# Convolution copies through memory on GpSimd's queue, with a block's write issued ahead of the reads of the block before

## The chip, the core and the metric

The kernel runs on one core of a Trainium2 chip, as one launch. The metric is the device time of one execution in microseconds; a run's figure is the median of several executions. SP, ACT and POOL can start DMAs, each in the order of its own instructions; an instruction that waits for a semaphore holds everything behind it on its engine.

## What is computed

A trunk of two layers over 256 positions of 1024 channels, in float32. Each layer is a SwiGLU FFN, a mixer and a second FFN, all with modulation and gates from a conditioning vector. The mixer of layer 0 is attention, that of layer 1 a convolution module, and the change lies in that one:

```python
def conformer_conv(h, w_pw1, b_pw1, w_dw, b_dw, ln_g, ln_b, w_pw2, b_pw2):
    u = h @ w_pw1 + b_pw1                      # 1024 -> 2048
    a, g = jnp.split(u, 2, axis=-1)
    u = a * jax.nn.sigmoid(g)
    u = depthwise_causal_conv(u, w_dw) + b_dw  # width 31, per channel
    u = jax.nn.silu(layer_norm(u, ln_g, ln_b))
    return u @ w_pw2 + b_pw2
```

(The call of the depthwise convolution is shortened here.)

## The kernel before

**Weights.** All weights come through one stream of loads, 512 KB (0.524 MB) each, 128 x 1024 float32, into a ring of six buffers `raw` (`RAW = 6`). `issue` (L191) starts a load on SP. `step` (L208) uses up the oldest one: for a weight, ACT rounds it to `whi` (L245, one load ahead of the step) and DVE subtracts to get `wlo` (L220); for a piece of the adaLN matrix DVE folds it into an accumulator (L284, L286). Then `step` issues the load six places on, which SP can start when the buffer is free. The pairs `whi`, `wlo` have a ring of six units (`RING = 6`), two loads to a unit; `high_part` (L233) refuses a unit while the one six places back still has uses, and the step then ends. `need(unit)` makes steps until a unit is there; `block()` (L258) makes as many as the quota of `take(n)` allows. A product with a weight is three matmuls per tile, hi.hi, lo.hi, hi.lo (L664 to L666).

**The convolution module** (`conv`, L1000) works on eight blocks of 128 channels. I number its loads from the first one of `pw1`: 0 to 15 are `pw1` (two per block), 16 to 23 `pw2`, 24 to 31 a piece of the adaLN matrix, from 32 on the weights of the last FFN. "Step n" uses up load n, and frees the buffer for load n + 6.

For a block b:

- `U(b)` (L1024): two products on TensorE, 48 matmuls of 256 columns, with a `need` and a `block()` ahead of them. Blocks 0 to 3 are done in another form (`UT`, `across`) before the loop.
- `glu(b)` (L1061): ACT takes the sigmoid of one half (L1065), DVE multiplies it into the row buffer `ub[b % 4]` (L1066), 288 columns with a margin of zeros.
- `spread(b)` (L1070): DMAs build `R[b]`. Its partitions 32 j to 32 j + 31 hold, for j = 0 to 3, the four groups of 32 channels side by side, shifted by j columns. That is 16 copies from on-chip memory to on-chip memory, each of 32 runs of 284 floats (1,136 bytes), half on SP and half on POOL. `R` has four buffers, so that `spread(b + 4)` waits for `C(b)`.
- `wide(b)` (L1017): POOL makes the weights `wd[b]` of the taps (three buffers, so that `wide(b + 3)` waits for `C(b)`).
- `C(b)` (L1079): 32 matmul instructions of 256 columns (64 rows in the trace) give the convolution, ACT moves it to `v` (L1089).
- `VT(b)` (L1093): two transposes of `v` into the accumulators `y` of the layer norm.

The order is written out by hand (L1149 to L1207); each engine executes its own instructions in that order. In the loop (L1178) it is U(b+4), glu(b+4), C(b), spread(b+4), wide(b+3), VT(b-1). After it come C(4) to C(7) with halves of 128 columns, interleaved with transposes, the moments, the norm, `swish` (four transposes and an activation), `put` (split into `hh` and `hl`) and the output product `O`. `run_sums(True)` makes the two column sums of an adaLN vector on TensorE (L340).

The last FFN's first loads are used up in the blocks after U(7): 32 to 35, where the ring of weight units refuses more.

Of the kernel before, what the change touches and what calls it, by code (L numbers as in the profile page):

```python
# [8 lines left out]
F32 = mybir.dt.float32  # L9
# [5 lines left out]
P = 128  # L15
# [41 lines left out]
class Trunk:  # L57
    def __init__(self, ctx, tc, a):
        self.tc, self.nc, self.a = tc, tc.nc, a

        def pool(name, bufs=1, **kw):
            return ctx.enter_context(tc.tile_pool(name=name, bufs=bufs, **kw))

        self.const = pool("const")
        self.tiny = pool("tiny", 2)
        pool("pad").tile([P, 256], F32, name="pad")
        self.rawp = pool("rawp", RAW)
        self.hlp = pool("hlp", RING)
        self.keep = pool("keep")
        self.two = pool("two", 2)  # L70
        self.ps = pool("ps", 1, space=bass.MemoryType.PSUM)
        self.vecs = {(l, s, k): Vec(l, s, k) for l in range(2) for s in range(3) for k in range(3)}
        self.sums, self.open, self.pend, self.naccs = [], [], [], 0
        self.phase = 0
        self.ss, self.rs, self.zs = {}, {}, {}
        self.quota = self.credit = 0
        self.plan()
# [189 lines left out]
    def take(self, n=None):  # L267
        self.quota = PUMP[self.phase] if n is None else n
# [731 lines left out]
    def conv(self, cp, before, after):  # L1000
        nc, a = self.nc, self.a
        b1, bdw = self.col["b1"], self.col["bdw"]
        lng, lnb = self.col["lng"], self.col["lnb"]
        cols, take = self.cols, self.take
# [5 lines left out]
        ub = [cp.tile([P, 288], F32, name=f"ub{i}") for i in range(4)]  # L1010
# [6 lines left out]
        def wide(b):  # L1017
            wd[b] = cp.tile([P, 8, 4, 32], F32, name="wd", tag="wd", bufs=3)
            nc.gpsimd.tensor_tensor(
                wd[b], self.w2[:, :, 4 * b : 4 * b + 4].unsqueeze(3).to_broadcast([P, 8, 4, 32]),  # L1020
                mask.unsqueeze(1).unsqueeze(1).to_broadcast([P, 8, 4, 32]), op=ALU.mult,
            )

        def U(b):  # L1024
            unit = self.pw1[b]
            self.need(unit)
            self.block()
            us[b] = self.bank("u")
            for s in range(2):
                out = us[b][:, s * T : s * T + T]  # L1030
                for k in range(KT):
                    cs = slice(k * 256 + s * P, k * 256 + s * P + P)
                    self.mm3(out, unit.hi[:, cs], unit.lo[:, cs], self.hh[:, k, :], self.hl[:, k, :], k == 0, k == KT - 1)
            unit.uses -= 1
# [26 lines left out]
        def glu(b):  # L1061
            ps = us.pop(b)
            u = ub[b % 4]
            sg = cp.tile([P, T], F32, name="sg", tag="sg", bufs=2)
            nc.scalar.activation(sg, ps[:, T:], AF.Sigmoid, bias=cols[:, b1 + 8 + b : b1 + 9 + b])  # L1065
            nc.vector.scalar_tensor_tensor(  # L1066
                u[:, 30:286], ps[:, 0:T], cols[:, b1 + b : b1 + b + 1], sg, op0=ALU.add, op1=ALU.mult
            )

        def spread(b):  # L1070

            u = ub[b % 4]
            R[b] = cp.tile([P, 4, 284], F32, name="R", tag="R", bufs=4)
            for g in range(4):
                for j in range(4):
                    eng = nc.sync if (g + j) % 2 else nc.gpsimd
                    eng.dma_start(R[b][32 * j : 32 * j + 32, g, :], u[32 * g : 32 * g + 32, j : j + 284])  # L1077

        def C(b, t0=0, n=T):  # L1079
            if ("v", b) not in us:  # L1080
# [85 lines left out]
        UT(w[1][:, 256:], 2, 1)  # L1166
        across(0, 1, e, 0), across(1, 1, e, 256)
        e = evac(w[1])
        glu(0), spread(0), wide(0)
        UT(w[3][:, 256:], 3, 1)  # L1170
        f = evac(w[3])
        across(2, 0, e, 0), across(2, 1, e, 256)
        glu(1), spread(1), wide(1)
        across(3, 0, f, 0), across(3, 1, f, 256)
        glu(2), spread(2), wide(2)
        glu(3), spread(3)
        take(PUMP_LOOP)
        for b in range(4):  # L1178
            U(b + 4)
            glu(b + 4)  # L1180
            C(b)
            spread(b + 4), wide(b + 3)
            if b:
                VT(b - 1)
                if b == 1:
                    nc.vector.tensor_tensor(b2, b2, gate, op=ALU.mult)
                else:
                    x = self.x[b - 2]
                    nc.vector.tensor_tensor(x, x, b2, op=ALU.add)
        nc.scalar.activation(warm, self.mhalf, AF.Silu)  # L1190
        self.block()
        C(4), wide(7), VT(3)
        self.need(self.pw2[3])
        take(5)
        C(5, 0, P), VT(4), self.block(), C(6, 0, P), VT(5, (0,)), C(7, 0, P), VT(6, (0,))
        C(5, P, P), VT(7, (0,)), moments(0), norm(0, 0), norm(0, 1)
        take(0)
        C(6, P, P), VT(5, (1,)), C(7, P, P), VT(6, (1,)), swish(0, 0), VT(7, (1,)), moments(1), put(0, 0)
        self.run_sums(True)
        swish(0, 1), norm(1, 0), put(0, 1), norm(1, 1)  # L1200
        O(0, 0), swish(1, 0), O(0, 1), put(1, 0), swish(1, 1), put(1, 1), take()
        O(0, 2), O(0, 3)
# [60 lines left out]
```

## Time and profile before

| | us |
|---|---|
| median of 3 runs | 1058.22 |
| lowest and highest run | 1056.94, 1062.69 |
| the profiled execution | 1057.27 |
| its span | 1055.5 |
| TensorE busy | 1020.3 (97%) |
| DVE, ACT, POOL busy | 785.3, 489.6, 86.8 |

The span is what the trace covers; the execution's own time is 1.77 us longer. All rows below are of that execution, in us from the span's start. The row of a matmul ends where its end is modelled, so rows on TensorE overlap a little. The convolution's U(4) begins at 759.88 us, and its first output product at 839.88 us.

### The profile page before, as it was taken

The page shows a single profiled execution, that of the slowest core. Times are in us where ns is not written, and L with a number is a line of the kernel's source. Part 1 is how long each engine was busy: PE and PEld are TensorE (multiplying, and loading weights), DVE is VectorE, ACT ScalarE, POOL GpSimd, SP SyncE. Part 2 cuts the span into 40 slices and gives each one's busy share as a digit, 9 for nine tenths or more (in the row PEclk, how much of TensorE's full clock was granted, in tenths as well). Part 3 has the DMA queues.
Part 4 walks back from the last instruction along what each step waited for, and adds up shares of the span by engine and source line. Part 5 has one row for each costly group of instructions (what it writes and reads, how often), then busy time and mean ns, then how long its engine had stood idle before and what let it go on. Part 6 is the DMA issues. An engine that isn't in the chain of part 4 may idle for free.

```text
span 1055.5 us, 14925 instructions
## 1 busy us (share of the span) xinstructions
PE 1020.3 (97%) x5510; PEld 826.7 (78%) x5510; DVE 785.3 (74%) x1165; ACT 489.6 (46%) x763; POOL 86.8 (8%) x149
## 2 busy tenths in 40 slices
PE   8999999999999999999999999999995899999998
PEld 5778787877776788878878878888984688888886
DVE  5679888978997798878578878776747669556643
ACT  3454444555685544444454444454621356434420
POOL 3000000002210000000020000000484200000000
PEclk9999999999999999999999999999998999999999
DMA  8989999948676399999739889894667427776711
GB/s 299 316 273 333 305 341 321 324 140 284 220 241 194 106 329 313 308 309 315 233 105 315 290 297 312 276 307 136 193 201 227 159 80 259 259 234 193 231 40 40
DMA packets 186812, 254.92 MB, mean 242 GB/s; under 512 B 10437, under 2 KB 136166, under 8 KB 186740
## 3 DMA queue, kind: packets, MB, share of 16 engines
q1 hardware_dynamic: 183856, 250.88, 72.1%
q0 software_dynamic: 2736, 3.04, 1.0%
q8 instruction: 43, 0.70, 0.3%
q14 instruction: 29, 0.24, 0.1%
q10 hardware_dynamic: 148, 0.06, 0.0%
HBM read 248.24 MB, written 1.05 MB: 236 GB/s over the span
## 4 chain that ended last, share of the span: by engine, by line
PE 79%; DVE 7%; DMA 5%; ACT 3%; issue 3%; POOL 2%; SPq 1%; DVEq 0%; ACTq 0%; POOLq 0%
PE u L666 14%; PE u L664 14%; PE u L665 14%; PE y L664 10%; PE y L666 10%; PE y L665 10%; DMA raw<-in_ffn_w_in_dram 2%; DMA raw<-in_ada_w_dram 2%; DVE wlo L220 2%; PE m L742 2%; ACT whi L245 1%; POOL R L1077 1%; PE m L1085 1%; ACT p L893 1%; DVE x L601 1%
## 5 line engine op out<-in xcount | busy, mean ns | idle before, releaser
L220 DVE TENSOR_TENSOR wlo<-raw,whi 128x1024 fp32r<-128x1024 f32 x320 | 389.2, 1244 | 51.1 <-ACT whi L245 50.8
L245 ACT ACTIVATE whi<-raw 128x1024 fp32r<-128x1024 f32 x320 | 329.1, 1055 | 178.1 <-DMA raw<-in_ffn_w_in_dram 96.2
L664 PE MATMUL u<-whi,hh 128*128 128x512 f32 x672 | 266.7, 397 | 1.2 <-ACT hh L587 1.2
L666 PE MATMUL u<-whi,hl 128*128 128x512 f32 x672 | 263.1, 391 | 0.0
L665 PE MATMUL u<-wlo,hh 128*128 128x512 f32 x672 | 261.8, 390 | 0.0
L286 DVE SCALAR_TENSOR_TENSOR acc<-raw,sc,acc 128x512 f32<-128x512 f32 x224 | 168.0, 750 | 6.7 <-DMA raw<-in_ada_w_dram 1.7
L666 PEld LDWEIGHTS u<-whi,hl 128*128 128x128 f32 x672 | 126.1, 188 | 29.6 <-DVE hl L588 1.7
L664 PEld LDWEIGHTS u<-whi,hh 128*128 128x128 f32 x672 | 126.2, 188 | 28.7 <-ACT hh L587 2.9
L665 PEld LDWEIGHTS u<-wlo,hh 128*128 128x128 f32 x672 | 126.4, 188 | 25.0
L664 PE MATMUL y<-whi,gh 128*128 128x512 f32 x352 | 138.5, 393 | 0.2 <-ACT gh L750 0.2
L666 PE MATMUL y<-whi,gl 128*128 128x512 f32 x352 | 137.3, 390 | 0.0
L665 PE MATMUL y<-wlo,gh 128*128 128x512 f32 x352 | 137.1, 389 | 0.0
L664 PE MATMUL y<-whi,hh 128*128 128x512 f32 (+1 forms) x256 | 96.9, 379 | 0.2 <-ACT hh L934 0.2
L666 PE MATMUL y<-whi,hl 128*128 128x512 f32 (+1 forms) x256 | 93.9, 367 | 0.0
L665 PE MATMUL y<-wlo,hh 128*128 128x512 f32 (+1 forms) x256 | 93.5, 365 | 0.0
L751 DVE TENSOR_TENSOR gl<-m,gh 128x512 fp32r<-128x512 f32 (+1 forms) x48 | 31.0, 647 | 83.7 <-ACT gh L750 83.5
L750 ACT ACTIVATE gh<-m 128x512 fp32r<-128x512 f32 (+1 forms) x48 | 27.0, 563 | 131.9 <-PE m L742 131.8
L712 ACT ACTIVATE sg<-u 128x256 f32<-128x256 f32 x84 | 32.1, 383 | 106.6 <-PE u L666 106.6
L664 PEld LDWEIGHTS y<-whi,gh 128*128 128x128 f32 x352 | 66.1, 188 | 15.7 <-ACT sg L712 1.7
L666 PEld LDWEIGHTS y<-whi,gl 128*128 128x128 f32 x352 | 66.1, 188 | 14.4 <-DVE gl L751 0.4
L665 PEld LDWEIGHTS y<-wlo,gh 128*128 128x128 f32 x352 | 66.1, 188 | 13.4
L620 POOL TENSOR_TENSOR r<-v,mhalf 128x1 f32<-128x1 f32 x12 | 6.6, 554 | 671.9 <-DVE v L619 671.9
(169 smaller groups left out, 944.6 us busy)
## 6 DMA issues: line engine op xcount, KB each, us to landing
raw<-in_ffn_w_in_dram SPq DMA_DIRECT2D x164, 512.0 KB, 5.1
raw<-in_ada_w_dram SPq DMA_DIRECT2D x144, 512.0 KB, 5.1
raw<-in_ffn_w_out_dram SPq DMA_DIRECT2D x88, 512.0 KB, 5.3
raw<-in_attn_w_qkv_dram SPq DMA_DIRECT2D x24, 512.0 KB, 4.9
raw<-in_conv_w_pw_dram SPq DMA_DIRECT2D x24, 512.0 KB, 5.1
raw<-in_ffn_w_in_dram SPq DMA_DIRECT2D x24, 256.0 KB, 5.7
raw<-in_attn_w_o_dram SPq DMA_DIRECT2D x8, 512.0 KB, 4.3
gate<-in_ada_b_dram SPq DMA_DIRECT2D x6, 512.0 KB, 6.7
```

Of the source, the lines that this page charges most:

```text
L220: (eng or nc.vector).tensor_tensor(lo, raw, hi.bitcast(F32), op=ALU.subtract)
L245: self.nc.scalar.activation(hi, self.like(self.raws[i], hi), AF.Copy)
L286: nc.vector.scalar_tensor_tensor(dst, raw[:, i, :], self.sc[:, k : k + 1], dst, op0=ALU.mult, op1=ALU.add)
L601: nc.vector.tensor_tensor(x[:, s], x[:, s], tmp, op=ALU.add)
L664: nc.tensor.matmul(out, lh, rh, start=start, stop=False)
L665: nc.tensor.matmul(out, lh, rl, start=False, stop=False)
L666: nc.tensor.matmul(out, ll, rh, start=False, stop=stop)
L712: nc.scalar.activation(sg, ps[:, 0:256], AF.Silu)
L742: nc.tensor.transpose(ps[:, o : o + P], g[:, t, k * P : k * P + P], self.ident)
L750: nc.scalar.activation(hi, src, AF.Copy)
L751: nc.vector.tensor_tensor(lo, src, hi.bitcast(F32), op=ALU.subtract)
L893: nc.scalar.activation(p[:, c0:c1], p[:, c0:c1], AF.Exp, bias=st[:, t : t + 1], scale=-1.0, accum_out=st[:, 2 + t : 3 + t],)
```

## The change

`spread(b)` now reads from memory. A new `park(b)` writes the row buffer (128 x 288) to a tile in DRAM, one of eight, on POOL; `spread(b)` is four DMAs on POOL, one for each shift j, each of which reads 32 x 4 x 284 floats, that is 128 runs of 1,136 bytes. A read waits for its write to land. `park(b + 1)` is issued ahead of `spread(b)`. SP has no part in it any more. The order of the blocks is rewritten for that: U(b+5) and glu(b+5) come ahead of C(b) in the loop, C(5) is done whole, one `block()` and one `take` go, and the column sums move ahead of the first `swish`.

```diff
+        self.dram = pool("dram", space=bass.MemoryType.DRAM)
...
+        drams = {}
+
+        def park(b):
+
+            drams[b] = self.dram.tile([P, 288], F32, name=f"d{b}")
+            nc.gpsimd.dma_start(drams[b], ub[b % 4])
+
         def spread(b):
 
-            u = ub[b % 4]
+            d = drams[b]
             R[b] = cp.tile([P, 4, 284], F32, name="R", tag="R", bufs=4)
-            for g in range(4):
-                for j in range(4):
-                    eng = nc.sync if (g + j) % 2 else nc.gpsimd
-                    eng.dma_start(R[b][32 * j : 32 * j + 32, g, :], u[32 * g : 32 * g + 32, j : j + 284])
+            for j in range(4):
+                src = bass.AP(tensor=d.tensor, offset=d.offset + j, ap=[[288, 32], [288 * 32, 4], [1, 284]])
+                nc.gpsimd.dma_start(R[b][32 * j : 32 * j + 32, :, :], src)
...
-        glu(0), spread(0), wide(0)
+        glu(0), park(0)
...
-        glu(1), spread(1), wide(1)
+        glu(1), park(1), spread(0), wide(0)
         across(3, 0, f, 0), across(3, 1, f, 256)
-        glu(2), spread(2), wide(2)
-        glu(3), spread(3)
+        glu(2), park(2), spread(1), wide(1)
+        glu(3), park(3), spread(2), wide(2)
         take(PUMP_LOOP)
+        U(4)
+        glu(4)
         for b in range(4):
-            U(b + 4)
-            glu(b + 4)
+            if b < 3:
+                U(b + 5)
+            park(b + 4), spread(b + 3)
+            if b:
+                wide(b + 2)
+            if b < 3:
+                glu(b + 5)
             C(b)
-            spread(b + 4), wide(b + 3)
             if b:
                 VT(b - 1)
...
         nc.scalar.activation(warm, self.mhalf, AF.Silu)
-        self.block()
+        spread(7), wide(6)
         C(4), wide(7), VT(3)
         self.need(self.pw2[3])
-        take(5)
-        C(5, 0, P), VT(4), self.block(), C(6, 0, P), VT(5, (0,)), C(7, 0, P), VT(6, (0,))
-        C(5, P, P), VT(7, (0,)), moments(0), norm(0, 0), norm(0, 1)
+        self.block()
+        C(5), VT(4), C(6, 0, P), VT(5), C(7, 0, P), VT(6, (0,))
         take(0)
-        C(6, P, P), VT(5, (1,)), C(7, P, P), VT(6, (1,)), swish(0, 0), VT(7, (1,)), moments(1), put(0, 0)
+        C(6, P, P), VT(7, (0,)), moments(0), norm(0, 0), norm(0, 1)
+        C(7, P, P), VT(6, (1,))
         self.run_sums(True)
+        VT(7, (1,)), swish(0, 0), moments(1), put(0, 0)
         swish(0, 1), norm(1, 0), put(0, 1), norm(1, 1)
```

SP's queue around U(4) to U(6), before; `raw` is a load (the first row is load 18), `R` a copy of `spread`:

```order
L205 DMA raw_6757<-in_conv_w_pw2_dram 128x1024
L1077 DMA R_6793<-ub0_6532 32x284 x8
L205 DMA raw_6813<-in_conv_w_pw2_dram 128x1024
L205 DMA raw_6819<-in_conv_w_pw2_dram 128x1024
L1077 DMA R_6856<-ub1_6533 32x284 x8
L1077 DMA R_6883<-ub2_6534 32x284 x8
L1077 DMA R_6905<-ub3_6535 32x284 x8
L205 DMA raw_6923<-in_conv_w_pw2_dram 128x1024
L205 DMA raw_6929<-in_conv_w_pw2_dram 128x1024
L205 DMA raw_6933<-in_conv_w_pw2_dram 128x1024
L205 DMA raw_6939<-in_ada_w_dram 128x2x512
L205 DMA raw_6943<-in_ada_w_dram 128x2x512
```

And now, from the same load on:

```order
L206 DMA raw_6759<-in_conv_w_pw2_dram 128x1024
L206 DMA raw_6798<-in_conv_w_pw2_dram 128x1024
L206 DMA raw_6804<-in_conv_w_pw2_dram 128x1024
L206 DMA raw_6880<-in_conv_w_pw2_dram 128x1024
L206 DMA raw_6886<-in_conv_w_pw2_dram 128x1024
L206 DMA raw_6890<-in_conv_w_pw2_dram 128x1024
L206 DMA raw_6896<-in_ada_w_dram 128x2x512
```

The 64 copies are gone from SP, and its loads follow each other.

POOL from the first block on, before (`ub` are the row buffers, `wd` the weights of the taps):

```order
L1077 DMA R_6793<-ub0_6532 32x284 x8
L1019 TENSOR_TENSOR wd_6810<-w2_4906,mask_6528 128x1024
L1077 DMA R_6856<-ub1_6533 32x284 x8
L1019 TENSOR_TENSOR wd_6873<-w2_4906,mask_6528 128x1024
L1077 DMA R_6883<-ub2_6534 32x284 x8
L1019 TENSOR_TENSOR wd_6900<-w2_4906,mask_6528 128x1024
L1077 DMA R_6905<-ub3_6535 32x284 x8
L1077 DMA R_7032<-ub0_6532 32x284 x8
L1019 TENSOR_TENSOR wd_7049<-w2_4906,mask_6528 128x1024
L1077 DMA R_7148<-ub1_6533 32x284 x8
```

And now, with the DRAM tiles `d0` to `d7`:

```order
L1076 DMA d0_6795<-ub0_6534 128x288
L1076 DMA d1_6841<-ub1_6535 128x288
L1084 DMA R_6843<-d0_6795 32x4x284 x4
L1020 TENSOR_TENSOR wd_6848<-w2_4908,mask_6530 128x1024
L1076 DMA d2_6858<-ub2_6536 128x288
L1084 DMA R_6860<-d1_6841 32x4x284 x4
L1020 TENSOR_TENSOR wd_6865<-w2_4908,mask_6530 128x1024
L1076 DMA d3_6870<-ub3_6537 128x288
L1084 DMA R_6872<-d2_6858 32x4x284 x4
L1020 TENSOR_TENSOR wd_6877<-w2_4908,mask_6530 128x1024
L1076 DMA d4_7013<-ub0_6534 128x288
L1084 DMA R_7015<-d3_6870 32x4x284 x4
```

Eight copies of a block have become one write and four reads, and the write of a block stands ahead of the reads of the block before.

TensorE at the end of the convolution, before: the first row is the second half of C(6), L1085 and L1099 are C and VT, L1122 the transposes of `swish`, L340 the column sums, the last row the first output product:

```order
L1085 MATMUL m_7654<-R_7282,wd_7432 32x128 x32
L1099 MATMUL y_7535<-ident_141,v_7498 128x128
L1085 MATMUL m_7689<-R_7415,wd_7490 32x128 x32
L1099 MATMUL y_7535<-ident_141,v_7537 128x128
L1122 MATMUL m_7724<-ident_141,z_7650 128x128 x4
L1099 MATMUL y_7535<-ident_141,v_7573 128x128
L340 MATMUL m_7745<-one_109,acc_7182 128x1 x4
L340 MATMUL m_7752<-one_109,acc_7308 128x1 x4
L1122 MATMUL m_7758<-ident_141,z_7652 128x128 x4
L664 MATMUL y_7776<-whi_6925,hh_117 128x512
```

And now (L1092, L1106, L1129 and L341 are those lines), from the second half of C(7):

```order
L1092 MATMUL m_7577<-R_7353,wd_7395 32x128 x32
L1106 MATMUL y_7457<-ident_143,v_7459 128x128
L341 MATMUL m_7612<-one_111,acc_7068 128x1 x4
L341 MATMUL m_7619<-one_111,acc_7186 128x1 x4
L1106 MATMUL y_7457<-ident_143,v_7496 128x128
L1129 MATMUL m_7627<-ident_143,z_7573 128x128 x4
L1129 MATMUL m_7646<-ident_143,z_7575 128x128 x4
L665 MATMUL y_7664<-whi_6882,hh_119 128x512
```

The column sums and the last VT have moved ahead of the first transposes of `swish`.

## Rows read from the trace of the kernel before

**Rows 1.** Stretches: from:to, length, busy (count) of PE, PEld, DVE, ACT, POOL; PEclk, DMA share, GB/s

```profile
760.00:810.00 50.00, 42.36 (x520) 33.52 (x518) 31.35 (x28) 10.69 (x15) 36.76 (x56) 0.97 0.69 211
770.00:780.00 10.00, 10.00 (x119) 8.25 (x118) 3.20 (x4) 0.96 (x2) 9.98 (x19) 1.00 0.44 107
780.00:790.00 10.00, 10.00 (x119) 8.25 (x118) 3.80 (x4) 4.28 (x7) 6.92 (x12) 1.00 0.91 298
800.00:810.00 10.00, 2.36 (x44) 1.17 (x36) 7.18 (x10) 0.00 (x0) 5.88 (x9) 0.86 0.80 272
810.00:820.00 10.00, 4.14 (x66) 3.49 (x66) 7.34 (x9) 5.39 (x7) 5.39 (x9) 0.63 0.80 251
840.00:850.00 10.00, 10.00 (x50) 8.25 (x49) 5.18 (x14) 4.52 (x12) 0.00 (x0) 1.00 0.00 0
880.00:900.00 20.00, 20.00 (x94) 16.57 (x93) 16.57 (x19) 11.44 (x15) 0.00 (x0) 1.00 0.98 325
```

**Rows 2.** Timeline of TensorE: start, length, line, what, count, idle before and releaser

```profile
759.88 0.36 PE L664 MATMUL u<-hh,whi 128*128 128x256 f32 x1
...
765.80 3.66 PE L1085 MATMUL m<-R,wd 128*32 128x256 f32 x64
...
798.70 3.66 PE L1085 MATMUL m<-R,wd 128*32 128x256 f32 x64
...
813.94 0.69 PE L1099 MATMUL y<-ident,v 128*128 128x128 f32 x2 [11.58 <-ACT v L1089]
...
821.52 0.69 PE L1099 MATMUL y<-ident,v 128*128 128x128 f32 x2 [3.44 <-ACT v L1089]
...
835.61 0.42 PE L1085 MATMUL m<-R,wd 128*32 128x128 f32 x7
```

**Rows 3.** Timeline of ACT in the loop and behind it

```profile
785.11 1.06 ACT L245 ACTIVATE whi<-raw 128x1024 fp32r<-128x1024 f32 x1 [14.15 <-DMA raw<-in_conv_w_pw_dram]
...
812.10 1.06 ACT L245 ACTIVATE whi<-raw 128x1024 fp32r<-128x1024 f32 x1 [21.86 <-DMA raw<-in_ffn_w_in_dram]
813.07 0.46 ACT L1065 ACTIVATE sg<-u,cols 128x256 f32<-128x256 f32 x1
813.42 0.47 ACT L1089 ACTIVATE v<-m,cols 128x256 f32<-128x256 f32 x1
```

**Rows 4.** Timeline of SP's queue: start and length of a run of DMA issues

```profile
762.46 18.23 SPq L1077 DMA_DIRECT2D R<-ub  x24
780.80 1.51 SPq L205 DMA_DIRECT2D raw<-in_conv_w_pw_dram  x3
...
803.50 0.51 SPq L205 DMA_DIRECT2D raw<-in_ffn_w_in_dram  x1
```

**Rows 5.** Line 1077, the copies: ns min/median/max of an issue, first and last start

```profile
L1077 SPq DMA_DIRECT2D R<-ub x64: 507/588/1639, 756.2 to 825.3; - x64
L1077 POOL DMA_DIRECT2D R<-ub x64: 496/496/532, 756.7 to 818.0; - x64
...
DMA to landing us min/median/max: 1.7/3.9/10.0
```

**Rows 6.** Timeline of DVE at the first blocks: ub(0), then steps 13 and 14

```profile
755.62 0.48 DVE L1066 SCALAR_TENSOR_TENSOR ub<-u,cols,sg 128x256 f32<-128x256 f32 x1 [1.08 <-ACT sg L1065]
756.02 2.35 DVE L220 TENSOR_TENSOR wlo<-raw,whi 128x1024 fp32r<-128x1024 f32 x2
```

**Rows 7.** DMA issues of the whole program: queue, count, size of one, median us to landing

```profile
raw<-in_ffn_w_in_dram SPq DMA_DIRECT2D x164, 512.0 KB, 5.1
...
R<-ub POOLq DMA_DIRECT2D x64, 35.5 KB, 4.5
...
out_dram<-x SPq DMA_DIRECT2D x4, 128.0 KB, 1.7
```

**Rows 8.** By line, as rows 5: POOL's loads of the taps, and wd

```profile
L987 POOL DMA_DIRECT2D tq<-in_conv_w_dw_dram x8: 548/551/618, 546.9 to 551.3; - x8
...
L1019 POOL TENSOR_TENSOR wd<-w,mask x8: 1920/1927/2941, 760.7 to 820.9; 128x1024 f32<-128x1024 f32 x8
```

**Rows 9.** Timeline of TensorE, as rows 2: the first output product

```profile
839.88 0.47 PE L664 MATMUL y<-whi,hh 128*128 128x512 f32 x1
```

## The prediction

> **What bounds the kernel now.** I read the cut into stretches first [rows 1]: TensorE is full in most of them, but works only 2.36 and 4.14 us of the two tens from 800 us, at a granted clock of 0.86 and 0.63. That is the end of the convolution. TensorE's own rows there [rows 2] show C(4) ending at 802.36 us, then a gap of 11.58 us that the arrival of v(3) ends, a second of 3.44 us for v(4), and the last half of C(7) ending at 836.03 us. A whole C takes 3.66 us in the loop; after 802.36 us three of them and a few transposes need 33.7 us, so the gaps and the low clock behind them are one cost.
>
> v(3) is an ACT row, and ACT shows why it was late [rows 3]: it stood 21.86 us before one rounding of a weight (whi, L245), until a load of ffn_w_in landed at 812.10 us; the sigmoid of U(7) and v(3) come straight behind it. Counting DVE's steps, that is load 32. SP's rows [rows 4] have its issue at 803.50 us, 8.6 us earlier. SP was late because it stood among R copies: 24 of them in one piece from 762.46 to 780.69 us, while loads 21 to 25, whose buffers DVE freed from 762 us on, wait until 780.80 us. ACT pays for that once before, with 14.15 us ahead of 785.11 us [rows 3], when TensorE still has U and C blocks in hand. A copy issued on SP takes 588 ns (median of 64 [rows 5]). While this goes on the DMA engines are not full: their share is 0.44 in the ten from 770 us [rows 1].
>
> **The change, part by part.**
>
> *SP loses its 64 copies*: 64 x 0.588 = 38 us of issue, and their waits. A load then follows the step that frees its buffer. The steps are the same ones at the same places (5, 2, 5, 5 and 4, set by the six weight buffers), so the pumped block that goes takes no load away.
>
> *TensorE*. Up to the end of C(4) its work only changes order: U(5) goes ahead of C(0), and so on. That part ran without a gap worth naming, from 759.88 to 802.36 us [rows 2], and stays. Behind it lie a whole C, four halves at 1.9 us (half of 3.66 and a start) and transposes, 0.37 us a pair and 0.2 us a single one: 3.66 + 4 x 1.9 + 4 x 0.37 + 2 x 0.2 = 13.1 us, so C(7) can end at 815.5 us instead of 836.03: **at most 20.5 us**. Nothing else on TensorE leaves.
>
> *How much of that the loads allow*. ACT now runs load 32's rounding, U(7)'s sigmoid and v(2) in this order, and TensorE wants v(2) at about 798.6 us (end of C(3)). Load 19 can go at about 757.3 us, when DVE ends the first of two subtractions [rows 6]. From there loads 19 to 32 (14 x 0.524 = 7.3 MB) and by then some seven writes and six blocks' reads (7 x 0.147 + 6 x 0.582 = 4.5 MB) must pass: 11.8 MB. At the best rate shown, 325 GB/s at a share of 0.98 [rows 1], that is 36 us, at 290 it is 41: load 32 lands at 794 to 798 us. With 1.06 us for the rounding and about half a us each for sigmoid and v [rows 3], v(2) is there at 796 to 800 us, and later by some latency where the chain step, issue, landing isn't full, at most a load's median time to landing, 5.1 us [rows 7]. The stall is 0 to 6 us; I take **3 us**, since each load is six steps ahead and so most of its latency is covered.
>
> *POOL* gets 8 writes and 32 reads for its 64 copies. No row has a POOL read of 1,136-byte runs from memory; the nearest is the tap load, also 128 runs per issue in the same three-level shape, 551 ns [rows 8], against 496 ns for a copy of 32 runs [rows 5]. I take 0.55. A block costs POOL 5 x 0.55 + 1.93 to 2.94 us (the wd product [rows 8]) = 4.7 to 5.7 us, and TensorE needs 9.6 us for one (a U from 759.88 to 765.80 us and a C of 3.66 us [rows 2]): hidden. The cover is the lead of the reads: spread(b+3) is issued in iteration b.
>
> *The round trip*. A read waits on POOL for its write to land. No row shows a POOL write; from below, 128 KB go out by SP in 1.7 us, from above POOL's copies land in 4.5 us [rows 7], at most 10.0 [rows 5]. With 4.5: ub(0) is written at 756.1 us [rows 6], d0 lands at 761.2, four issues end at 763.4, R(0) is there at 768 us; C(0) now comes at 771.5 us, because U(5) stands ahead of it. Cost nothing; if the reads took 10 us it would be 2 us. The other tight place is R(7): spread(7) must wait for C(3), which ends at 798.3 + 3, and for d7; issues and landing bring it to about 811 us, and C(7) is wanted at 809 + 3. The wd products of blocks 6 and 7 stand behind it on POOL; C(6) would be the one to feel that, by some tenths.
>
> *The tail*. The two column sums now stand ahead of the first four transposes of the norm instead of behind them. Before, the first O follows C(7) by 3.85 us [rows 9]. Now 0.1 + 2 x 1.0 + 0.2 us go first, and from the transposes to hh and hl I reckon 2.5 us: about 4.8 us, so **+1 us** (0 to 1.5).
>
> *Later stages*. In the ten from 840 us the DMA engines move nothing [rows 1]: the ring of loads is full. The changed kernel meets that point with the same steps done, so the last FFN moves forward as a whole.
>
> Sum: -20.5 + 3 + 1 = -16.5 us. The profiled execution took 1057.27 us, so 1040.8; the median of the runs shown is 0.95 us above that one, so about **1041.5 us**.
>
> One thing speaks against this. The copies move between queues, but all bytes still use the same DMA engines. With a share of 0.44 in a ten in which SP is blocked, the rows say that the queue was the limit and the engines were not. The Trainium skill ("DMA: Bandwidth & Descriptors", Issuing engines are not separate DMA queues) says that DMAs of all issuing engines run on the same 16 DMA engines and interleave, and that issuing from several saves only the sequencer's time to start them, usually small beside the transfer. By that rule the loads would gain nothing, and the sum would be +1 us. The trace speaks against its word small here: SP's issues alone are 38 us of one stage.
>
> **The rivals.**
>
> *A. The engines are the bound after all.* From 760 to 810 us the core moved 211 GB/s [rows 1]. If that were all that this mixture allows, 11.8 MB need 56 us, load 32 lands at 813 us as now, and nothing is won: 1058 to 1060 us. For it: the copies' runs are short. Against: 298 GB/s in the ten from 780 us, beside copies, and the share of 0.44 before. (This is what the rule of the Trainium skill named above, in "DMA: Bandwidth & Descriptors", would do here.)
>
> *B. Half of it.* Loads land in 8.6 us, as load 32 did, and the rate is nearer 260 GB/s: load 32 at 803 to 806 us, so a stall of 7 to 11 us instead of 3: 1046 to 1050 us.
>
> *C. POOL becomes the bound (slower).* Its chain is 40 issues of d us, six wd products ahead of the last copy (14 us), landing (4.5) and the halves from C(7) on (6.1): 756 + 40 d + 14 + 4.5 + 6.1, or 781 us + 40 d. With d = 0.55 this is 803 us, under the 818 that I expect; from d = 0.95 POOL decides, at d = 1.4 the gain is gone, and at d = 2.0 C(7) ends at 861 us and the kernel takes about 1083 us. For it: POOL had no such long three-level read before. Against: 551 ns for 128 runs [rows 8], and the copies stay at 496 to 532 ns while DVE works [rows 5].
>
> *D. More than forecast*: no stall and no dearer tail, 1036 to 1038 us.
>
> **How the numbers follow.** Forecast (1038 to 1045 us) 0.60, B 0.17, D 0.07, A 0.08, C 0.08. A measurement of this kernel tells about 0.5%, 5 us, from no change. Faster is the forecast, B and D, 0.84; same is A, 0.08; slower is C, 0.08. The range takes in D, the forecast and B, from 1036 to 1051 us; A and C, 0.16, lie outside.
>
> **What would show it.** Right: SP's rows in the stage hold loads only; the stretch from 760 us shows a DMA share of 0.8 or more; ACT's longest wait before whi falls from 21.86 us to under 8; the gaps of 11.58 and 3.44 us give way to one of some 3 us at the transposes of v(2), or none; the granted clock stays at 1.00; C(7) ends near 818 us. A is right if the share is near 1 and load 32 still lands near 812 us. C is right if POOL's issues take over 0.95 us and C waits for R. The tail is right if the first O follows C(7) by about 4.8 us. The prediction is wrong if C(0) waits for R(0) by more than 2 us, or if gaps appear after 840 us that were not there.

## The result, and the profile after

| | before | changed |
|---|---|---|
| median, us | 1057.58 (1054.70 to 1062.69, 4 runs) | 1046.83 (1044.06 to 1048.11, 4 runs) |
| the profiled execution | 1057.27 | 1048.11 |
| its span | 1055.5 | 1046.3 |

The ratio is 0.989, with an interval of 0.9846 to 0.9933: 10.8 us faster, a gain of 1.1% that is clear of the noise. The time is 5.3 us above the forecast and inside the range. The mechanism is the one described; the stretch from U(4) to the end of C(7) gave 12.6 us where 17.5 were expected (20.5 less the stall of 3), and 2.7 us were lost behind it.

The stretches of the changed kernel, to be held against [rows 1] (columns: stretch, its length, busy us of TensorE, weight loads, DVE, ACT and POOL, granted clock, DMA share, GB/s):

```profile
760.00:810.00 50.00, 45.14 (x536) 34.92 (x540) 35.96 (x36) 14.84 (x22) 30.90 (x41) 0.97 1.02 297
800.00:810.00 10.00, 6.19 (x80) 3.07 (x84) 4.75 (x6) 4.29 (x8) 4.70 (x6) 0.83 1.04 340
820.00:830.00 10.00, 9.21 (x161) 8.08 (x161) 6.28 (x17) 3.91 (x11) 1.11 (x2) 0.86 0.13 50
830.00:840.00 10.00, 10.00 (x41) 8.09 (x41) 4.44 (x12) 3.01 (x8) 0.00 (x0) 0.80 0.01 2
```

The DMA share of the first 50 us is 1.02 where it was 0.69, at 297 GB/s instead of 211: the DMA engines are now full. TensorE works 6.19 us of the ten from 800 us instead of 2.36. A dip of the clock stands at 820 to 840 us (0.86 and 0.80), at the first output product. In the kernel before, that product ran at 1.00 (the ten from 840 us in [rows 1]).

TensorE's rows from U(4) over the first C to the first output product (the counterpart of [rows 2] and [rows 9]; L1092 is C, L1106 VT, L341 the column sums, L1129 the transposes of `swish`, L665 and L666 the output product):

```profile
760.56 0.37 PE L665 MATMUL u<-hh,whi 128*128 128x256 f32 x1
...
772.24 3.66 PE L1092 MATMUL m<-R,wd 128*32 128x256 f32 x64
...
795.44 3.66 PE L1092 MATMUL m<-R,wd 128*32 128x256 f32 x64
...
803.81 0.69 PE L1106 MATMUL y<-ident,v 128*128 128x128 f32 x2 [4.71 <-ACT v L1096]
804.43 4.78 PE L1092 MATMUL m<-R,wd 128*32 128x256 f32 x64
...
814.88 1.95 PE L1092 MATMUL m<-R,wd 128*32 128x128 f32 x64 [1.34 <-POOL wd L1020]
...
817.84 1.96 PE L1092 MATMUL m<-R,wd 128*32 128x128 f32 x64 [0.63 <-POOL wd L1020]
...
822.12 1.96 PE L1092 MATMUL m<-R,wd 128*32 128x128 f32 x64
...
824.17 1.84 PE L341 MATMUL m<-one,acc 128*128 128x1 f32 x16
...
827.85 0.80 PE L665 MATMUL y<-whi,hh 128*128 128x512 f32 x1 [0.79 <-DVE hh L1145]
828.44 0.63 PE L666 MATMUL y<-wlo,hh 128*128 128x512 f32 x1
828.87 0.63 PE L667 MATMUL y<-whi,hl 128*128 128x512 f32 x1
```

C(0) does not wait for R(0). The gaps of 11.58 and 3.44 us have become one of 4.71 us, at the transposes of v(2), and the C behind it, C(4), takes 4.78 us instead of 3.66 at a clock that has fallen (0.83 in the ten from 800 us). Two halves then wait 1.34 and 0.63 us for the products `wd` of blocks 6 and 7. C(7) ends at 824.08 us. The first output product comes 3.77 us later, and its first twelve matmuls follow each other at 0.43 us, against 0.23 us at the full clock.

ACT, for [rows 3]:

```profile
770.44 1.06 ACT L246 ACTIVATE whi<-raw 128x1024 fp32r<-128x1024 f32 x1 [2.43 <-DMA raw<-in_conv_w_pw_dram]
...
801.97 1.06 ACT L246 ACTIVATE whi<-raw 128x1024 fp32r<-128x1024 f32 x1 [15.98 <-DMA raw<-in_ffn_w_in_dram]
802.93 0.46 ACT L1066 ACTIVATE sg<-u,cols 128x256 f32<-128x256 f32 x1
803.29 0.83 ACT L1096 ACTIVATE v<-m,cols 128x256 f32<-128x256 f32 x2
```

The same load 32 still ends ACT's longest wait, 15.98 instead of 21.86 us, at 801.97 instead of 812.10 us. The sigmoid of U(7) and v(2), v(3) come behind it as before.

SP, for [rows 4], and POOL around blocks 4, 6 and 7:

```profile
768.12 16.68 SPq L206 DMA_DIRECT2D raw<-in_ada_w_dram  x8
789.76 23.69 SPq L206 DMA_DIRECT2D raw<-in_ffn_w_in_dram  x8
```

```profile
782.52 0.56 POOL L1076 DMA_DIRECT2D d<-ub  x1 [0.47 <-issue]
785.06 2.18 POOL L1084 DMA_DIRECT2D R<-d  x4 [1.97 <-DMA d<-ub]
...
804.21 0.60 POOL L1076 DMA_DIRECT2D d<-ub  x1 [8.95 <-DVE ub L1067]
804.80 2.18 POOL L1084 DMA_DIRECT2D R<-d  x4
...
810.70 2.20 POOL L1084 DMA_DIRECT2D R<-d  x4 [1.77 <-issue]
812.90 4.78 POOL L1020 TENSOR_TENSOR wd<-w,mask 128x1024 f32<-128x1024 f32 x2
```

SP holds loads alone. Load 32 is issued at 789.76 us, 13.7 us sooner than before, but it takes 12.2 us to land, where the median of a load is 5 us. Its first packet moves at 795.04 us. POOL's reads cost 0.55 us each, as taken. The end of POOL's work shows the chain behind the stall: `ub(7)` late at 804.2 us, then d7, the reads of R(7) at 810.70, and only then the last two `wd`.

The landing times in the page's list of DMAs (KB each, median us to landing):

```profile
R<-d POOLq DMA_DIRECT2D x32, 142.0 KB, 7.5
d<-ub POOLq DMA_DIRECT2D x8, 144.0 KB, 6.5
```

**Where the 9.2 us of the two spans went.** U(4) begins 0.68 us later (760.56 for 759.88 us); in the profiles of the experiments below it begins between 758.15 and 759.94 us, so this part need not come from the change. From there to the end of C(7) it is 63.5 us instead of 76.15: -12.6. From there to the end of the span it is 222.2 us instead of 219.5: +2.7, of which 12 matmuls of the first output product at the low clock make about 12 x 0.2 = 2.4.

### The profile page after: what moved, and what is told of

Same layout as the page of the kernel before. It is cut to its first block, busy times and chain, and to the rows that moved or that the text cites. A ratio compares the mean times of both kernels' runs of the same rounds, so it can differ in the third digit from the quotient of the medians.

```text
span 1046.3 us, 14593 instructions
## 1 busy us (share of the span) xinstructions
PE 1019.1 (97%) x5446; PEld 824.1 (79%) x5446; DVE 784.1 (75%) x1165; ACT 489.2 (47%) x762; POOL 76.2 (7%) x125
## 4 chain that ended last, share of the span: by engine, by line
PE 80%; DVE 7%; DMA 4%; ACT 4%; issue 3%; POOL 1%; SPq 0%; DVEq 0%; ACTq 0%; POOLq 0%
PE u L667 15%; PE u L665 15%; PE u L666 15%; PE y L665 10%; PE y L667 10%; PE y L666 9%; DVE wlo L221 3%; DMA raw<-in_ada_w_dram 2%; PE m L743 2%; ACT whi L246 1%; DMA raw<-in_ffn_w_in_dram 1%; DMA raw<-in_attn_w_qkv_dram 1%; PE m L1092 1%; DVE x L602 1%; PE m L644 1%
## 5 line engine op out<-in xcount | busy, mean ns | idle before, releaser
L665 PE MATMUL u<-whi,hh 128*128 128x512 f32 x672 | 266.7, 397 | 1.2 <-ACT hh L588 1.2
L666 PE MATMUL u<-wlo,hh 128*128 128x512 f32 x672 | 261.8, 390 | 0.0
L287 DVE SCALAR_TENSOR_TENSOR acc<-raw,sc,acc 128x512 f32<-128x512 f32 x224 | 171.5, 765 | 10.5 <-DMA raw<-in_ada_w_dram 5.6
L665 PEld LDWEIGHTS u<-whi,hh 128*128 128x128 f32 x672 | 126.2, 188 | 28.5 <-ACT hh L588 2.9
L666 PEld LDWEIGHTS u<-wlo,hh 128*128 128x128 f32 x672 | 126.4, 188 | 25.0
L665 PE MATMUL y<-whi,gh 128*128 128x512 f32 x352 | 138.5, 393 | 0.2 <-ACT gh L751 0.2
L666 PE MATMUL y<-wlo,gh 128*128 128x512 f32 x352 | 137.1, 389 | 0.0
L665 PE MATMUL y<-whi,hh 128*128 128x512 f32 (+1 forms) x256 | 97.9, 383 | 1.0 <-DVE hh L1145 0.8
L666 PE MATMUL y<-wlo,hh 128*128 128x512 f32 (+1 forms) x256 | 94.5, 369 | 0.0
L665 PEld LDWEIGHTS y<-whi,gh 128*128 128x128 f32 x352 | 66.1, 188 | 15.6 <-ACT sg L713 1.7
L666 PEld LDWEIGHTS y<-wlo,gh 128*128 128x128 f32 x352 | 66.1, 188 | 13.4
L665 PEld LDWEIGHTS y<-whi,hh 128*128 128x128 f32 x256 | 49.4, 193 | 12.5 <-issue 4.0
```

The source lines that it names most:

```text
L287: nc.vector.scalar_tensor_tensor(dst, raw[:, i, :], self.sc[:, k : k + 1], dst, op0=ALU.mult, op1=ALU.add)
L665: nc.tensor.matmul(out, lh, rh, start=start, stop=False)
L666: nc.tensor.matmul(out, lh, rl, start=False, stop=False)
```

## The experiments

Two kinds: which part of the change brings the gain (four kernels that take it apart), and what bounds the changed kernel (six kernels that move or leave out work). As a common measure I use the stage, from the first matmul of U(4) to the end of C(7): 76.15 us before, 63.5 us in the changed kernel. "The gap at v" is TensorE's wait at the transposes of v(2), where ACT brings v late.

### The order alone

The changed order of U, glu, reads, `wd`, C and the end, with the sixteen direct copies of a block on SP and POOL:

```diff
         def park(b):
-            drams[b] = self.dram.tile([P, 288], F32, name=f"d{b}")
-            nc.gpsimd.dma_start(drams[b], ub[b % 4])
+            pass
...
-            for j in range(4):
-                src = bass.AP(...)
-                nc.gpsimd.dma_start(R[b][32 * j : 32 * j + 32, :, :], src)
+            for g in range(4):
+                for j in range(4):
+                    (nc.sync if (g + j) % 2 else nc.gpsimd).dma_start(R[b][32 * j : 32 * j + 32, g, :], u[32 * g : 32 * g + 32, j : j + 284])
```

> The changed order of U, glu, reads, wide, C and the end, but with the sixteen direct copies of a block, half on SP and half on POOL, as before; no tile in memory. Theory (SP's blocking is the cost and the order only serves to hide the round trip): SP has its 64 copies, load 32 is as late as before, 1054 to 1060 us. Rival (the new order is what gained, since U stands a block further ahead and covers the waits): 1045 to 1049 us.

Measured: 1059.23 us (10 runs), ratio 1.0004 [0.9986, 1.0022]. The order by itself is worth nothing, and the theory's 1054 to 1060 us holds. Its profile is of its slowest execution (1063.50 us), so only its pattern is read. Its TensorE rows at the end:

```profile
807.62 0.69 PE L1105 MATMUL y<-ident,v 128*128 128x128 f32 x2 [8.27 <-ACT v L1095]
808.24 6.58 PE L1091 MATMUL m<-R,wd 128*32 128x256 f32 x64
818.99 6.79 PE L1091 MATMUL m<-R,wd 128*32 128x256 f32 x64 [3.80 <-DMA R<-ub]
```

and SP's:

```profile
758.80 17.62 SPq L1083 DMA_DIRECT2D R<-ub  x24
776.54 1.49 SPq L206 DMA_DIRECT2D raw<-in_conv_w_pw_dram  x3
...
809.93 20.12 SPq L1083 DMA_DIRECT2D R<-ub  x24
```

SP stands 17.6 us in front of 24 copies again, as in [rows 4], and 20 us later on. In this execution load 32's rounding starts 46.2 us after U(4), 6 us sooner than before, and the gap at v is 8.27 us; what it costs less, C(5) to C(7) pay in waiting for copies and at a low clock (6.58 and 6.79 us for a C instead of 3.66).

### The route alone

The kernel before in its own order, with the write and the four reads right behind each other on POOL:

```diff
-            u = ub[b % 4]
+            d = self.dram.tile([P, 288], F32, name=f"d{b}")
+            nc.gpsimd.dma_start(d, ub[b % 4])
             R[b] = cp.tile([P, 4, 284], F32, name="R", tag="R", bufs=4)
-            for g in range(4):
-                for j in range(4):
-                    eng = nc.sync if (g + j) % 2 else nc.gpsimd
-                    eng.dma_start(R[b][32 * j : 32 * j + 32, g, :], u[32 * g : 32 * g + 32, j : j + 284])
+            for j in range(4):
+                src = bass.AP(...)
+                nc.gpsimd.dma_start(R[b][32 * j : 32 * j + 32, :, :], src)
```

> The kernel before, in its own order, with only the route changed: in place of its sixteen copies each block is written to memory and read back by four reads, all five on GpSimd's queue and right behind one another, so that POOL waits for each write to land. With the run of the new order alone this is the other half of the change. Theory (the route through memory brings the gain, the order only keeps the round trip off the path): SP holds loads alone and load 32 lands near 802 us as in the changed kernel, but POOL stands about 5 us per block before its reads, R(4) to R(7) and the products behind them come some 5 us later for a TensorE that is one block less ahead; gaps before C of 3 to 10 us in all on top of the changed kernel's: 1049 to 1057 us. Rival (the lead of the writes is not needed, R is two or more blocks ahead anyway): 1044 to 1048 us, as the changed kernel. Second rival (the order is needed for the route to win anything): 1058 us or more.

Measured: 1065.46 us (4 runs), ratio 1.0076 [1.0053, 1.0099], 0.8% slower than before. The theory's 1049 to 1057 us is missed, and the second rival holds. POOL, in its rows, waits for each write:

```profile
765.41 0.60 POOL L1074 DMA_DIRECT2D d<-ub  x1
771.39 2.19 POOL L1078 DMA_DIRECT2D R<-d  x4 [5.38 <-DMA d<-ub]
...
782.31 0.60 POOL L1074 DMA_DIRECT2D d<-ub  x1
788.73 2.19 POOL L1078 DMA_DIRECT2D R<-d  x4 [5.82 <-DMA d<-ub]
...
827.41 2.19 POOL L1078 DMA_DIRECT2D R<-d  x4 [5.74 <-issue]
```

and TensorE waits once for R and three times for the `wd` that stand behind the reads on POOL:

```profile
769.80 5.35 PE L1086 MATMUL m<-R,wd 128*32 128x256 f32 x64 [3.88 <-DMA R<-d]
...
803.56 5.35 PE L1086 MATMUL m<-R,wd 128*32 128x256 f32 x64 [3.08 <-POOL wd L1020]
...
814.51 5.24 PE L1086 MATMUL m<-R,wd 128*32 128x256 f32 x64 [5.23 <-POOL wd L1020]
...
831.59 3.51 PE L1086 MATMUL m<-R,wd 128*32 128x128 f32 x64 [8.08 <-POOL wd L1020]
```

These four gaps are 20.3 us, and each C behind one runs at a low clock (5.24 to 5.35 us instead of 3.66, the half 3.51 instead of 1.95). Load 32's rounding starts at 801.09 us, 41.2 us after U(4), as in the changed kernel (41.4) and 11 us sooner than before (52.2). So **the route frees the loads, and the order pays for the round trip**:

| ratio to the kernel before | order of before | new order |
|---|---|---|
| direct copies | 1 | 1.0004 |
| through memory | 1.0076 | 0.989 |

### The reads on SP

```diff
-                nc.gpsimd.dma_start(R[b][32 * j : 32 * j + 32, :, :], src)
+                nc.sync.dma_start(R[b][32 * j : 32 * j + 32, :, :], src)
```

> The changed kernel with the four reads of a block issued on SP; the write stays on POOL. Theory (the kernel before lost its time because SP stood before copies while buffers for loads were free): SP now waits for the block's write to land and for the R buffer ahead of loads, load 32 lands at 806 us or later, the gap at v(2) or v(3) is 8 us or more: 1051 to 1060 us. Rival (the queue does not matter, all DMAs share the engines, and what was won is the smaller number of copies): load 32 near 802 us as in the changed kernel, 1045 to 1049 us.

Measured: 1046.54 us (4 runs), ratio 0.9884 [0.9861, 0.9907]: the changed kernel's time. My theory falls; the rival has the time, but not by its way. Load 32 lands much sooner, at 793.96 us (35.8 us after U(4)), and the wait has gone over to R(5). TensorE and SP:

```profile
807.73 5.69 PE L1092 MATMUL m<-R,wd 128*32 128x256 f32 x64 [6.66 <-DMA R<-d]
```

```profile
759.18 8.07 SPq L1084 DMA_DIRECT2D R<-d  x12
...
788.88 7.58 SPq L206 DMA_DIRECT2D raw<-in_ffn_w_in_dram  x5
796.57 11.64 SPq L1084 DMA_DIRECT2D R<-d  x12
```

SP now issues 32 reads (median 430 ns) where it had 64 copies (588 ns), and stands 24.5 us before them in all. The reads of R(5) stand behind five loads on SP and start at 796.57 us. The queue alone is thus not what won: with either queue the DMA engines are full (share 1.00 from 760 to 810 us here) and somebody waits. What the two kernels at 1046.5 to 1046.8 us share, and the direct copies lack, is that five DMAs do the work of sixteen. The engines' work did not get less by it: the write adds bytes, and reckoned for a share of 1 the engines moved 291 GB/s in the changed kernel (297 at 1.02) and 306 before (211 at 0.69). No kernel here makes on-chip copies of 128 runs each, four to a block, so that the trip through memory is needed for the smaller number is not shown.

### Direct copies on POOL alone

As the order alone, with all sixteen copies on POOL (`nc.gpsimd.dma_start` in both loops).

> The changed kernel without the trip through memory: no write, and spread makes the 16 direct copies of 32 runs of before, all on POOL. SP holds loads only, as in the changed kernel. Theory (freeing SP is the gain, and memory is only what lets four issues do for sixteen): POOL's chain is 128 x 0.496 + 8 x 2.0 = 80 us, so the last copies are issued at about 834 us less two wd, C(7) ends at 840 to 848 us, 1062 to 1070 us: slower than before, with POOL as the bound. Rival (memory traffic is what the changed kernel pays for): 4.5 MB instead of 5.8 MB, load 32 lands some 4 us sooner, and the time is 1040 to 1045 us.

Measured: 1077.40 us in one run, worse than either theory's figure. Freeing SP is not enough: with 128 copies at about 0.5 us POOL becomes the bound, and `wd` waits behind them. POOL also stands 11.2 us between copies until earlier ones have landed, which the theory's sum of 80 us did not have:

```profile
813.04 6.25 PE L1091 MATMUL m<-R,wd 128*32 128x256 f32 x64 [14.71 <-POOL wd L1020]
```

Load 32 lands at 796.38 us here, 36.6 us after U(4): with SP free and few copies under way it comes in time, and it no longer matters. This is rival C of the prediction, brought about by the number of issues.

### Half of the reads

Two of the four reads of a block are left out, so this kernel does not compute the convolution; it only shows what their bytes cost:

```diff
-            R[b] = cp.tile([P, 4, 284], F32, name="R", tag="R", bufs=4)
-            for j in range(4):
+            R[b] = rb[b % 4]
+            for j in range(2):
```

> The changed kernel with two of the four reads of each block left out (shifts 2 and 3; those halves of the R buffers are cleared once, so the convolution is not the reference's). 8 x 0.291 MB fewer bytes, all waits between writes and reads as before. Theory (bytes through full DMA engines set when load 32 lands): up to load 32 some 1.75 MB less at 297 GB/s, 6 us, so ACT rounds load 32 at about 796 us instead of 801.97, the gap at v(2) is 0 to 1 us, 1038 to 1042 us. Rival (latency of the chain step, issue, landing, not bytes): the rounding stays within 1.5 us of 801.97 and the time at 1045 to 1048 us.

Measured: 1035.84 us (4 runs), ratio 0.9785 [0.9766, 0.9803]; the stage takes 56.2 us. ACT's row for load 32:

```profile
793.35 1.06 ACT L246 ACTIVATE whi<-raw 128x1024 fp32r<-128x1024 f32 x1 [9.28 <-DMA raw<-in_ffn_w_in_dram]
```

It lands 34.7 us after U(4) instead of 41.4, so 6.7 us sooner, and the gap at v is gone, as the theory had it; the time is 2 us under its figure. Six blocks' reads pass ahead of load 32 in both kernels; half of them are 6 x 2 x 142 KB = 1.74 MB, which at the 297 GB/s of the changed kernel's stage take 5.9 us. Bytes through full DMA engines are thus most of what load 32 waits for in the changed kernel.

### U(7)'s weight steps moved behind

```diff
         for b in range(4):
+            if b == 2:
+                take(0)
             if b < 3:
                 U(b + 5)
...
                 VT(b - 1)
+                if b == 2:
+                    take(4)
+                    self.block()
...
-        self.block()
-        C(5), VT(4), C(6, 0, P), VT(5), C(7, 0, P), VT(6, (0,))
+        take(6)
+        C(5), VT(4), self.block(), C(6, 0, P), VT(5), C(7, 0, P), VT(6, (0,))
```

> The changed kernel, with the steps of U(7)'s block moved behind glu(7) and VT(1) (four of them, loads 27 to 30) and the last five behind C(5). So ACT no longer rounds load 32 ahead of U(7)'s sigmoid and v(2), and DVE no longer folds loads 27 to 31 ahead of ub(7). Theory (the DMA engines are full, load 32 lands late, and what stands behind it on ACT and DVE pays): the gap of 4.71 us at the transposes of v(2) and the 1.34 and 0.63 us of waiting for wd go, C(4) runs at full clock, C(7) ends at 816 to 818 us instead of 824.08; 1038 to 1041 us against 1046.8. Rival (POOL's round trip through memory is late by itself): the gap at v(2) goes, but C(6) and C(7) still wait for wd or R, C(7) ends at 820 to 822 us; 1043 to 1045 us.

Measured: 1041.59 us (4 runs), ratio 0.9837 [0.9819, 0.9855]; the stage takes 59.9 us. Load 32's rounding no longer stands ahead of sg(7) and v(2), and the gap there is gone, though load 32 is rounded only at 805.80 us, 47 us after U(4) (the first of three roundings in this row):

```profile
805.80 2.94 ACT L246 ACTIVATE whi<-raw 128x1024 fp32r<-128x1024 f32 x3
```

A new gap, a wait for R as the rival had it, takes half of the gain on TensorE, and the time lies between the two figures:

```profile
811.31 1.95 PE L1092 MATMUL m<-R,wd 128*32 128x128 f32 x64 [3.38 <-DMA R<-d]
```

### All five steps behind C(5)

U(7)'s block makes none, five steps stand behind C(5) and VT(4), and four are left to the output products:

```diff
         for b in range(4):
+            if b == 2:
+                take(0)
...
-        self.block()
-        C(5), VT(4), C(6, 0, P), VT(5), C(7, 0, P), VT(6, (0,))
+        take(5)
+        C(5), VT(4), self.block(), C(6, 0, P), VT(5), C(7, 0, P), VT(6, (0,))
```

> Edit: U(7)'s block takes no weight steps; the five that stood there (27 to 31, among them the one of load 32's buffer) go behind C(5) and VT(4), and four steps of the last FFN stay for the blocks of the output products. Theory (what is left of the stall is only ACT standing before a load that comes late, and the 3.38 us gap of the run with U(7)'s steps moved comes from loads that compete with the reads of R(6) and R(7)): no gap at v(2), no gap over 1 us at C(6) and C(7), C(7) ends 56 to 57 us after U(4) begins (changed kernel 63.5, U(7)'s steps moved 59.9), 1037 to 1039 us. Rival (the loads are bound by the engines from one end to the other, so each step moved back must be paid later): C(7) ends as early, but the four steps left over show as gaps in the output products or at the start of the last FFN, and the time is 1041 us or more.

Measured: 1040.23 us (4 runs), ratio 0.9828 [0.981, 0.9846]. TensorE has no gap in the stage, which takes 55.3 us (758.15 us to the end of the first row below), the shortest of all; but its rows later show what was pushed back:

```profile
811.45 1.95 PE L1092 MATMUL m<-R,wd 128*32 128x128 f32 x64
...
851.67 1.09 PE L644 MATMUL m<-ident,z 128*128 128x128 f32 x8 [0.95 <-DVE z L628]
...
856.65 0.50 PE L665 MATMUL u<-whi,hh 128*128 128x512 f32 x1 [1.14 <-ACT hh L659]
```

Theory and rival each have half of it: the stage is as the theory said, and the four steps left over are paid in the last FFN (2.1 us). The five moved steps are paid as well: they keep DVE busy up to 813.1 us, the norm behind them is late, and the output products begin 4.99 us after C(7) instead of 3.77. The total misses 1037 to 1039 us by 1.2.

### Two steps more in the middle

As the last, with two steps behind C(3) and VT(2):

```diff
                 VT(b - 1)
+                if b == 3:
+                    take(2)
+                    self.block()
```

> The run with the five steps behind C(5), and two more weight steps behind C(3) and VT(2), so that two instead of four stay for the output products. Theory (what that run lost behind C(7), a gap of 2.1 us of TensorE between 850 and 860 us, comes from the four steps left over, and two of them fit where DVE and ACT are idle): the gap there is under 1 us, C(7) still ends 55 to 58 us after U(4) begins, 1037.5 to 1039.5 us. Rival (the two loads that these steps release compete with the reads of R(7), as with U(7)'s steps moved): a gap of 1.5 us or more at the first half of C(7), and 1040 to 1042 us.

Measured: 1037.86 us (4 runs, 1037.13 to 1043.16), ratio 0.9822 [0.9791, 0.9852]. The gaps of the last FFN are gone, as the theory said, and the gap at the first half of C(7) is there, as the rival said:

```profile
809.21 1.95 PE L1092 MATMUL m<-R,wd 128*32 128x128 f32 x64 [1.50 <-DMA R<-d]
```

Each run of this and the last two kernels (1037.13 to 1043.16 us) is under each run of the changed kernel (1044.06 to 1048.11), although the intervals of their ratios just touch its own (0.9855 and 0.9852 against 0.9846). Among the three the runs overlap, so none is shown to be the best.

### The end as before

```diff
-        C(7, P, P), VT(6, (1,))
+        C(7, P, P), VT(6, (1,)), swish(0, 0), VT(7, (1,)), moments(1), put(0, 0)
         self.run_sums(True)
-        VT(7, (1,)), swish(0, 0), moments(1), put(0, 0)
```

> The changed kernel with the end of the convolution as before: the first four transposes of the norm ahead of the last VT, and the column sums behind the first put. Theory (the order of the tail lets the clock fall to 0.50 for the first output products): the twelve matmuls of the first O run at 0.23 us each again instead of 0.43, and the time is 2 to 3 us less, 1044 to 1045 us. Rival (the clock falls because of the gaps at wd and v(2) some us earlier): the clock stays at about 0.5 there, and the time within 1 us of the changed kernel.

Measured: 1047.04 us (4 runs), ratio 0.9885 [0.9864, 0.9905], no difference from the changed kernel, so the rival has the time. The output product starts 4.7 us after C(7) instead of 3.77, but here at the full clock, as the theory said; its stage was 2 us longer in the profiled execution, in which the gap at v is wider:

```profile
805.00 0.69 PE L1106 MATMUL y<-ident,v 128*128 128x128 f32 x2 [6.52 <-ACT v L1096]
```

The same end, on the kernel with all five steps behind C(5):

> The edit of the run before and, besides, the end in the order of the kernel before (first four transposes of the norm ahead of the two column sums). Theory (the low clock of the first output products comes from the gap of TensorE between C(7) and the transposes of the norm, which the new order makes longer): these products run at a clock of 1.00 and the time is 1 to 3 us under that of the run before. Rival (the order of the end decides nothing, as the first run of it alone had it): within 1 us of the run before, and the clock of the first output products is low or full in either.

Measured: 1042.71 us (4 runs), ratio 0.9852 [0.9836, 0.9867], 2.5 us more than with the new end, where neither theory (1 to 3 us less) nor rival (within 1 us) had it; the two intervals overlap, so the loss is not shown. The first output product comes 7.16 us after C(7), and with the low clock:

```profile
816.64 0.63 PE L1129 MATMUL m<-ident,z 128*128 128x128 f32 x4 [2.20 <-DVE z L1122]
...
822.34 0.63 PE L667 MATMUL y<-whi,hl 128*128 128x512 f32 x1
```

The theory falls: the first output products run low under the old end here, and at full clock under the new end with U(7)'s steps moved and with all five behind C(5). So the order of the end does not decide the clock, and no length of gap that I see in the rows does. It stays open.

## Why the prediction was right, and where its sizes were off

The measured time lies in the band of rival B (1046 to 1050 us, chance 0.17) and not in the forecast's own (1038 to 1045). The mechanism held and most of its sizes came out too good, nearly all on one side; the range held them because it took in B.

Of the signs named ahead, these came: loads alone on SP, a DMA share of 1.02, one gap at the transposes of v(2) for the two, and no wait of C(0). These did not: ACT's longest wait is 15.98 us and not under 8, the clock did not stay at 1.00, C(7) ends at 824.08 us and not near 818, and the first output product follows it by 3.77 us and not by 4.8. ACT's wait was a poor sign. ACT stands before the rounding from 785.99 us on, but C(2), whose v(2) stands behind it, ends only at 795.14 us, and TensorE feels only the part behind the end of C(3) at 799.10 us, 4.71 us.

**The bound** (load 32, ACT held by its rounding, TensorE waiting for v): right. In each kernel in which load 32 came sooner, or its rounding stood later, the gap at v shrank or went.

**SP's 64 copies**: right as a cost, too narrow as a reason. That SP stood before copies did delay the loads, and SP is now free. But with the reads on SP the time is the same, and with all direct copies on POOL it is 18 us worse than before (one run). With five DMAs to a block either queue will do; with sixteen, half of them on SP or all on POOL, the gain is lost. The prediction counted SP's issues, 38 us, but put the gain down to their leaving SP.

**TensorE's upper gain, at most 20.5 us**: right to 0.4 us. The kernel without a gap in the stage takes 55.3 us, 20.9 less than before.

**The stall, 3 us (0 to 6)**: mis-sized. It was 4.71 us, and C(4) behind it lost 1.1 us to the clock, which the sum had not counted. Load 32 was put at 794 to 798 us and came at 801.97. The term that was mis-sized is the 11.8 MB. They end with load 32, but the loads behind it are on the same engines before it has landed. From 758 to 802 us, 44 us at 288 GB/s, 12.7 MB passed. By the sizes of the trace's packets these are the 11.9 MB of the prediction's list, 0.1 MB left of load 18, and 0.6 MB of loads 33 and later: their packets are of 1,024 bytes, load 32 has 512 of them, and some 1,100 had passed when it landed. By this rate, load 32 would without these 0.8 MB have come at about 799 us, and the stall been some 2 us (an estimate). The rate itself, 290 to 325, was about right.

**POOL, 0.55 us an issue, hidden**: right in the loop. **The round trip, nothing**: right for C(0). Writes took 6.5 and reads 7.5 us to land, not 4.5, and in the loop the lead covered them; without it, as the route alone shows, TensorE loses some 20 us. **The products of blocks 6 and 7, some tenths**: mis-sized, 1.34 + 0.63 = 2.0 us, since `ub(7)` was itself late behind load 32, and POOL then stood 1.77 us more ahead of the reads of R(7).

**The tail, +1 us**: wrong in sign, 3.77 instead of 3.85 us, and a cost that the prediction did not have stood behind it: 2.4 us of low clock in the output product.

Added up: 1.7 and 1.1 us of stall and clock, some 1.5 us for `wd`, 0.7 us for U(4), 2.4 us less 1.1 for the end make 6.3 us on top of the 1040.8 of the sum, 1047.1; the profiled execution took 1048.11, and 1 us has no term.

**The rule weighed against the change** ("DMA: Bandwidth & Descriptors", Issuing engines are not separate DMA queues): in the changed kernel the share is 1.02, and moving the reads from POOL to SP changes nothing (1046.83 and 1046.54 us). The Trainium skill's rule that all issuing engines feed the same 16 DMA engines agrees with these numbers. A copy of 35.5 KB takes 0.5 to 0.6 us to issue and 3.9 us to land [rows 5], and 128 of them on POOL end 18 us behind the kernel before (one run). The Trainium skill's remark that the time to start a DMA is usually small beside the transfer thus agrees with the trace for one copy, and does not carry over to many on one queue.

**The rivals.** A fell: load 32 came 10 us sooner. Yet what A feared is now true one step on, the engines are full. B was nearest in size: a late load and a stall above 3 us, at 1046 to 1050 us; but load 32 (801.97 us) and the stall (4.71 us) are under its figures, and its 260 GB/s were not what made the load late. C was avoided by the count of issues, 40 at 0.55 us. D is what the kernels with moved steps reach, 1037.9 us at best.

## What to carry to other kernels

Count the issues of each in-order queue before asking which queue: five DMAs of 128 runs for sixteen of 32 freed the loads, whichever queue carried them. A route with a round trip paid here only when the program order gave each write a block's lead over its reads; measure route and order apart, since here one alone won nothing, the other alone lost, and the two together won. Once the DMA engines are full, look at what sits in front of the critical instruction on an engine that waits for a load, and move that work instead.

## What was not expected of the hardware

- A load takes 12.2 us to land and a write of 144 KB 6.5 us while the DMA share is at 1.0; load 32 took 8.6 us in the kernel before.
- The granted clock at the first output product was low (0.43 us from one matmul to the next) in the profiles of the changed kernel, of half of the reads, of the reads on SP, of the two steps in the middle, and of the old end with five steps behind C(5); it was full (0.23 us) in U(7)'s steps moved, all five behind C(5), and the old end alone. Of the two levels these are 1.2 and 2.4 GHz. Between C(7) and this product TensorE's gaps are 0.66 to 0.99 us long in the kernels at the full clock and 0.66 to 2.20 us in those at the low one; the cause stays open.
